# One full-height value product for the 16 meta keys of an attention head, and a 128-wide spread of the reciprocal sums

## The chip, the core and the metric

The kernel runs on one core of a Trainium2 chip. A core has a matrix engine (TensorE, PE in the rows; PEld is its loading of stationary operands), a vector engine (DVE), a scalar engine (ACT), a general engine (GpSimd, POOL) and a queue engine that issues transfers (SP). Matrix products are written to PSUM; all else lies in SBUF, 128 partitions wide. The metric is the device time of one execution in microseconds (us); less is better.

## The reference

A layer of a streaming encoder: 2048 tokens of width 1024, with 16 learned meta tokens in front (2064 rows). After a norm, one projection feeds eight heads of a recurrence (RWKV-7) and eight heads of forgetting attention; both results go through an output projection, and a gated feed-forward network with a short convolution follows. The change touches the attention alone:

```python
def block(args):                       # 128 queries at a time
    q_i, c_i, pos_i = args
    s = jnp.einsum('bhqd,bhkd->bhqk', q_i, k) + c_i[..., None] - c[:, :, None, :]
    s = jnp.where(kpos[None, :] <= pos_i[:, None], s, -jnp.inf)
    p = jax.nn.softmax(s, axis=-1)
    return jnp.einsum('bhqk,bhkd->bhqd', p, v)
...
o = o * jax.nn.sigmoid(og.astype(f32))
```

## The kernel before

All large products take each fp32 operand as two parts, a rounded high part (type fp32r) and the rest (low), and sum three products: high by high, high by low, low by high. The program is written in blocks, but the order of the instructions on each engine is made by a list scheduler when the program is built; it is fixed then. Instructions of one engine run in that order, and wait for the others by semaphores.

Attention is built three times. `at(0, True)` and `at(1, False)` take queries of the first half, with two buffers for a head's keys and values; `at2` takes the eight later query blocks, with one buffer. In each, `run` goes over eight heads. `load_head` (L876) brings a head's keys, queries and values; `vs` is the value tile, [keys, key block, 128], with the high part of the 64 value columns in its left half and the low part in its right half. Key block 0 holds the 16 meta keys, the others 128 keys each. `softmax` makes the unnormalised probabilities P of 128 queries. `value` (L971) takes a pair of query blocks (N = 256 columns, or 272 with the 16 meta queries): for every key block it transposes P on TensorE into `pt` (L995), splits it into `ph` on ACT (L1003) and `pl` on DVE (L1004), and adds two products to `o`, `ph` by `vs` and `pl` by `vs` (L1008). `value` runs 64 times: 8 heads by 2, 2 and 4 pairs. For block 0 both operands have 16 partitions only, so these products use 16 rows of the array.

Behind the products, the reciprocal of the softmax sum, a column per query, is brought into row form: GpSimd copies it 64 wide into `E` (L1019), TensorE transposes `E` into a PSUM tile of the scores' kind, `rp` (L1020), and ACT copies that to `rb` (L1023), which multiplies the output gate `og`.

While attention runs, the scheduler puts feed-forward and output-projection products between its own: helper line L1083 with the tiles `pp`, `ww_hi`, `ww_lo`, and `pj` (L203 to L205) of the last input projections.

Of the kernel before, what the change touches and what calls it, by code (L numbers as in the profile page):

```python
# [7 lines left out]
F32 = mybir.dt.float32  # L8
F32R = mybir.dt.float32r
AF = mybir.ActivationFunctionType  # L10
ALU = mybir.AluOpType
# [51 lines left out]
def pools(*args):  # L63

    *ps, where = args
    return lambda shape, tag, bufs=1, dt=F32: ps[where.get(tag, -1)](shape, tag, bufs, dt)
# [789 lines left out]
def attention(K, ctx, name, phases, bufs, banks):  # L856


    nc = K.nc
    sp = pools(*(Pool(K.tc, ctx, name + i, side="right") for i in "ab"), dict.fromkeys(("kl", "kq", "cb", "raw", "vs"), 0))  # L860
    ps = pools(*(Pool(K.tc, ctx, f"{name}ps{i}", PSUM, side="right") for i in range(3)), {"s": 0, "pt": 1})
    nhead, nP, nph, W, nraw, masks, kve = bufs
    ns, npt, no = banks
# [3 lines left out]
    NQ = max(sum(16 if i < 0 else 128 for i in qt) for bl in phases for qt in bl)  # L867
    pmask = False

    if masks:  # L870
        idr, cmr = (sp([128, 128], t, dt=F32R) for t in ("idr", "cmr"))
        nc.scalar.copy(idr, K.ident)
        nc.scalar.copy(cmr, K.cmask)

    def load_head(h, qa, nk_all):
        p_, hh = divmod(h, 2)  # L876
        r = slice(64 * hh, 64 * hh + 64)
        kl = sp([128, NK], "kl", nhead, F32R)[:, :nk_all]
        kq = sp([128, NK + NR], "kq", nhead, F32R)
        kh, qs = kq[:, :nk_all], kq[:, NK : NK + nk_all - qa]  # L880
        cb = sp([128, NK], "cb", nhead)[:, :nk_all]
        nc.sync.dma_start(cb, K.cd[h : h + 1, :nk_all].to_broadcast([128, nk_all]))
        raw_tile = lambda: sp([128, W], "raw", nraw)
        sub = (nc.vector if kve else nc.gpsimd).tensor_sub
        for a, b, both in pieces(qa, nk_all):
            n, t, u = b - a, slice(a, b), slice(a - qa, b - qa)
            raw = raw_tile()[:, : n * (1 + both)].rearrange("p (i t) -> p i t", t=n)
            for j in range(2):
                nc.sync.dma_start(raw[64 * j : 64 * j + 64], K.qk[p_, r, 0 : 1 + both, t])
            nc.scalar.copy(kh[:, t], raw[:, 0])  # L890
            sub(kl[:, t], raw[:, 0], kh[:, t].bitcast(F32))  # L891
            if both:
                nc.scalar.copy(qs[:, u], raw[:, 1])
                nc.gpsimd.tensor_sub(qs[64:128, u], raw[64:128, 1], qs[64:128, u].bitcast(F32))  # L894
        nt = (nk_all - 16) // 128 + 1
        vs = sp([128, (NK - 16) // 128 + 1, 128], "vs", nhead, F32R)
        for j in [0, *range(1, nt, W // 64)]:
            p, js = (16, 1) if j == 0 else (128, min(W // 64, nt - j))
            raw = raw_tile()[:p, : 64 * js].rearrange("p (j d) -> p j d", d=64)
            k0 = keys(j)[0]  # L900
            nc.sync.dma_start(raw, K.vn[k0 : k0 + p * js, 64 * h : 64 * h + 64].rearrange("(j p) d -> p j d", p=p))
            t = vs[:p, j : j + js]
            nc.scalar.copy(t[:, :, 0:64], raw)
            nc.gpsimd.tensor_sub(t[:, :, 64:128], raw, t[:, :, 0:64].bitcast(F32))
        og = sp([64, NR], "og", min(nhead, 2))[:, : nk_all - qa]
        nc.sync.dma_start(og, K.og[p_, r, qa:nk_all])
        return kh, kl, qs, cb, vs, og, qa

    def pieces(qa, nk):

        out = []
        for lo, hi, w in ((0, qa, W), (qa, nk, W // 2)):
            m = -(-(hi - lo) // w)
            w = -(-(hi - lo) // (16 * m)) * 16 if m else w
            out += [(a, min(a + w, hi), lo == qa) for a in range(lo, hi, w)]
        return out
# [52 lines left out]
    def keys(j):  # L969
        return (0, 16) if j == 0 else (16 + 128 * (j - 1), 128)  # L970

    def value(hd, qt, soft):

        vs, qa = hd[4], hd[6]
        nqs = [16 if i < 0 else 128 for i in qt]
        Ps, inv = zip(*soft)
        q0 = 0 if qt[0] < 0 else 16 + 128 * qt[0]
        N = sum(nqs)
        per = 2 if N <= 256 else 1
        shape = [128, per, 512 // per]  # L980
        o = ps([128, 512], "o", no)[:, :N]
        nt = qt[-1] + 2
        j = 0
        while j < nt:
            js = [j] if j == 0 else list(range(j, min(j + per, nt)))
            pt = ps(shape, "pt", npt)
            kn = keys(j)[1]
            ph, pl = sp(shape, "ph", nph, F32R), sp(shape, "pl", nph, F32R)
            cols = []
            for x, jj in enumerate(js):  # L990
                k0, kn = keys(jj)
                c0 = 0
                for P, i, nq in zip(Ps, qt, nqs):
                    if jj <= i + 1:
                        nc.tensor.transpose(pt[:kn, x, c0 : c0 + nq], P[:nq, k0 : k0 + kn], K.ident[:nq, :nq])  # L995
                    c0 += nq
                cols.append(sum(nq for i, nq in zip(qt, nqs) if jj > i + 1))
            if len(set(cols)) == 1:
                views = [(slice(0, len(js)), cols[0])]
            else:  # L1000
                views = [(slice(x, x + 1), c) for x, c in enumerate(cols)]
            for xs, c in views:
                nc.scalar.copy(ph[:kn, xs, c:N], pt[:kn, xs, c:N])  # L1003
                nc.vector.tensor_sub(pl[:kn, xs, c:N], pt[:kn, xs, c:N], ph[:kn, xs, c:N].bitcast(F32))  # L1004
            for x, jj in enumerate(js):
                c = cols[x]
                for y, pp in enumerate((ph, pl)):
                    nc.tensor.matmul(o[:, c:N], vs[:kn, jj], pp[:kn, x, c:N], start=jj == 0 and y == 0,  # L1008
                                     stop=jj == nt - 1 and y == 1)
            j += len(js)  # L1010
        o2 = sp([64, NQ], "o2", min(nhead, 2))[:, :N]
        nc.scalar.copy(o2, o[64:128])
        nc.vector.tensor_tensor(o2, o2, o[0:64], op=ALU.add)

        rp = ps([128, 512], "s", ns)[:64, :N]
        c0 = 0
        for r, nq in zip(inv, nqs):
            e = sp([128, 64], "E", 2)[:nq]
            nc.gpsimd.tensor_scalar(e, r.to_broadcast([nq, 64]), 1.0, 0.0, op0=ALU.mult, op1=ALU.add)  # L1019
            nc.tensor.transpose(rp[:, c0 : c0 + nq], e, K.ident[:nq, :nq])  # L1020
            c0 += nq
        rb = sp([64, NQ], "rb", min(nhead, 2))[:, :N]
        nc.scalar.copy(rb, rp)  # L1023
        og = hd[5][:, q0 - qa : q0 - qa + N]
        nc.gpsimd.tensor_tensor(og, og, rb, op=ALU.mult)
        nc.vector.tensor_tensor(og, o2, og, op=ALU.mult)

    def finish(hd, h, qt, soft, last):
        value(hd, qt, soft)
        if last:  # L1030
            p_, hh = divmod(h, 2)
            og, qa = hd[5:]
            nc.sync.dma_start(K.yd[4 + p_, 64 * hh : 64 * hh + 64, qa : qa + og.shape[1]], og)
# [176 lines left out]
def tail(K, ctx, at, c0):  # L1210
# [7 lines left out]
    with ExitStack() as c1:  # L1218
        gA = pools(*(Pool(tc, c1, f"ff{i}", side="left") for i in "ABCD"), {"acc": 0, "xh": 1, "xl": 2})
        bank = lambda shape: pA(shape, "pp", 3)  # L1220
        cvA = lambda: gA([128, 512], "cv", 5)
        early = [F.group(*g, dict(x=gA, a=gA, z=gA, out=bank, up=bank, ytag="x", abufs=1, parts=WHOLE, small=KC,
                                  cv=cvA, sq=cvA, stage=lambda i: lambda c: cvA())) for g in FGROUPS[:2]]
        early[0].parts = PARTS
        early[0].small = KC // 2
        early[1].small = 0
        F.w_o(early[0])
        at(1, False)
        c0.close()
        with ExitStack() as c2:  # L1230
            attention(K, c2, "at2", [[[2 * i, 2 * i + 1] for i in range(4, 8)]], (1, 4, 2, 352, 2, 0, 0), (2, 2, 1))(0, False)
        pR = Pool(tc, late, "ffpR", PSUM, side="right")
        bankR = lambda shape: pR(shape, "pr", 5)
        F.mlp(early[0])()
        F.w_o(early[1])
        rest = F.mlp(early[1], 8, bankR)
        R = Pool(tc, late, "ffR", side="right")

        def stage(i):
            t = R([128, KC, 514], "yh" if i else "yl")  # L1240
            return lambda c: t[:, c]

        gs = [F.group(*g, dict(x=R, a=R, abufs=1, out=bankR, up=bank, ytag="y", stage=stage, parts=WHOLE, small=KC,
                                   sq=lambda: R([128, 512], "sqv", 1))) for g in FGROUPS[2:]]
        F.w_o(gs[0])
        rest()
# [61 lines left out]
```

## Time and profile before

| | |
|---|---|
| median of 3 runs | 3463.3 us (3452.35 to 3463.97) |
| the profiled execution | 3458.59 us; its span 3456.7 us |
| mean granted TensorE clock in it | 0.989 |
| TensorE busy | 3351.8 us, 97% of the span |
| DVE, ACT, POOL busy | 2296.5, 1650.9, 1151.2 us |

The span runs from the first to the last instruction; 1.9 us of the profiled execution lie around it. Sums below are made against the profiled execution, and 4.7 us is what it lies below the median.

### The profile page before, as it was taken

To read this page: it belongs to the slowest core of one execution; us is meant where nothing else is said; L and a number is where in the kernel's file an instruction comes from. 1 tells how busy PE (TensorE), PEld (TensorE's weight loads), DVE (VectorE), ACT (ScalarE), POOL (GpSimd) and SP (SyncE) were. 2 spreads that over 40 slices of the span, in tenths; PEclk is the share of its full clock that TensorE was granted. 3 is DMA by queue.
4 is the path that set the end of the run, shared out by engine and by line. 5 is a ranking of instruction groups with operands and counts; after the bars stand their busy time and mean duration, and the time that the engine had idled before them with its cause. 6 is when DMAs were issued, how large, how long until landed. Compare 5 with 4: busy or idle time off the path is not lost.

```text
span 3456.7 us, 62711 instructions
## 1 busy us (share of the span) xinstructions
PE 3351.8 (97%) x23323; PEld 2950.0 (85%) x23323; DVE 2296.5 (66%) x4849; ACT 1650.9 (48%) x3426; POOL 1151.2 (33%) x2029
## 2 busy tenths in 40 slices
PE   7999999999999998999999999999999999999999
PEld 7889889988988987999999998888887888878887
DVE  5655666576566656887778776776664666646665
ACT  4543444554344466765666665555333333333332
POOL 4441113344111256744444344332214221132111
PEclk9999999999999999999999999999999999999999
DMA  4565343356534264333332353232324323232322
GB/s 113 120 140 148 96 108 87 102 121 146 147 96 104 79 180 135 114 99 103 93 89 82 92 160 94 91 100 86 121 92 146 104 92 98 88 120 93 97 92 92
DMA packets 352890, 376.60 MB, mean 109 GB/s; under 512 B 169112, under 2 KB 281992, under 8 KB 351560
## 3 DMA queue, kind: packets, MB, share of 16 engines
q1 hardware_dynamic: 352392, 372.52, 37.6%
q8 instruction: 184, 3.01, 0.4%
q14 instruction: 122, 1.00, 0.1%
q0 software_dynamic: 192, 0.07, 0.0%
HBM read 302.22 MB, written 70.27 MB: 108 GB/s over the span
## 4 chain that ended last, share of the span: by engine, by line
PE 50%; DMA 2%; issue 1%; POOL 1%; DVE 1%; ACT 1%; SPq 0%; POOLq 0%; ACTq 0%; DVEq 0%
PE pp L1083 30%; PE pr L1083 12%; PE o L1008 3%; PE pt L995 2%; PE s L946 1%; DMA raw<-d_qk 1%; PE s L948 1%; POOL kl L891 0%; DVE ww_lo L82 0%; DMA cb<-d_cd 0%; PE s L1020 0%; ACT ph L1003 0%; ACT P L965 0%; DVE P L939 0%; POOL kq L894 0%
## 5 line engine op out<-in xcount | busy, mean ns | idle before, releaser
L82 DVE TENSOR_TENSOR ww_lo<-ww_raw,ww_hi 128x1024 fp32r<-128x1024 f32 (+1 forms) x304 | 373.9, 1239 | 237.4 <-PE pp L1083 128.4
L81 ACT CAST ww_hi<-ww_raw 128x1024 fp32r<-128x1024 f32 (+1 forms) x304 | 307.4, 1024 | 392.9 <-PE pp L1083 147.9
L1083 PE MATMUL pp<-xh,ww_hi 128*128 128x512 f32 (+2 forms) x1952 | 431.4, 354 | 13.0 <-ACT xh L1144 4.7
L1083 PE MATMUL pp<-xl,ww_hi 128*128 128x512 f32 (+2 forms) x1952 | 431.7, 351 | 0.0
L1083 PE MATMUL pp<-xh,ww_lo 128*128 128x512 f32 (+2 forms) x1952 | 430.6, 351 | 0.0
L1083 PEld LDWEIGHTS pp<-xh,ww_hi 128*128 128x128 f32 x1952 | 325.4, 190 | 69.1 <-ACT xh L1144 9.8
L1083 PEld LDWEIGHTS pp<-xl,ww_hi 128*128 128x128 f32 x1952 | 328.7, 189 | 52.9
L1083 PEld LDWEIGHTS pp<-xh,ww_lo 128*128 128x128 f32 x1952 | 325.3, 189 | 46.8
L1166 POOL TENSOR_SCALAR c<-c,pc 128x1 f32<-128x1 f32 x220 | 82.4, 375 | 582.4 <-ACT c L1163 580.9
L1004 DVE TENSOR_TENSOR pl<-pt,ph 128x512 fp32r<-128x512 f32 (+4 forms) x416 | 220.6, 538 | 67.7 <-ACT ph L1003 63.4
L1003 ACT CAST ph<-pt 128x512 fp32r<-128x512 f32 (+4 forms) x416 | 189.3, 468 | 144.9 <-PE pt L995 105.8
L939 DVE CUSTOM_DVE_ANT_0 P<-cb,s 16x16 f32<-16x16 f32 (+8 forms) x360 | 183.0, 520 | 73.8 <-PE s L948 45.1
L1178 POOL TENSOR_TENSOR zl<-cv,zh 128x512 fp32r<-128x512 f32 (+1 forms) x110 | 122.2, 1111 | 300.0 <-ACT zh L1177 276.6
L1191 DVE TENSOR_TENSOR acc<-acc,pr 128x512 f32<-128x512 f32 x240 | 164.4, 688 | 81.3 <-PE pr L1083 76.9
L995 PE MATMUL pt<-cst,P 128*128 128x128 f32 (+2 forms) x1224 | 198.6, 276 | 3.1 <-DVE pl L1004 1.5
L1008 PE MATMUL o<-ph,vs 128*128 128x256 f32 (+3 forms) x640 | 188.5, 302 | 11.2 <-ACT ph L1003 6.8
L1160 ACT ACTIVATE cv<-pp,pc 128x510 f32<-128x510 f32 (+1 forms) x220 | 151.8, 691 | 84.0 <-PE pp L1083 82.3
L1008 PE MATMUL o<-pl,vs 128*128 128x256 f32 (+3 forms) x640 | 174.7, 290 | 5.0 <-DVE pl L1004 4.4
L89 POOL TENSOR_TENSOR wi<-sq,kx 128x320 fp32r<-128x320 f32 (+2 forms) x48 | 48.3, 1007 | 390.8 <-ACT kx L88 291.7
L203 PE MATMUL pj<-xah,w_hi 128*128 128x384 f32 x480 | 164.9, 344 | 1.7 <-ACT xah L194 1.7
L205 PE MATMUL pj<-xah,w_lo 128*128 128x384 f32 x480 | 163.3, 340 | 0.4 <-DVE w_lo L82 0.4
L204 PE MATMUL pj<-xal,w_hi 128*128 128x384 f32 x480 | 163.0, 340 | 0.0
(386 smaller groups left out, 8557.4 us busy)
## 6 DMA issues: line engine op xcount, KB each, us to landing
ww_raw<-in_fin_dram SPq DMA_DIRECT2D x176, 512.0 KB, 3.5
ww_raw<-in_fout_dram SPq DMA_DIRECT2D x88, 512.0 KB, 3.6
w_raw<-in_wt_dram SPq DMA_DIRECT2D x60, 512.0 KB, 3.7
xv<-d_var SPq DMA_DIRECT2D x32, 384.0 KB, 6.0
ww_raw<-in_wo_dram SPq DMA_DIRECT2D x24, 512.0 KB, 3.4
raw<-d_qk SPq DMA_DIRECT2D x112, 88.0 KB, 2.6
cb<-d_cd SPq DMA_DIRECT2D x8, 1032.0 KB, 8.2
out_dram<-acc SPq DMA_DIRECT2D x32, 256.0 KB, 2.9
```

Source lines behind the costliest of these rows:

```text
L81: nc.scalar.copy(hi, raw)
L82: nc.vector.tensor_sub(lo, raw, hi.bitcast(F32))
L203: nc.tensor.matmul(p, wh[:, c, :M], xh[:, c, :n], start=c == 0, stop=False)
L204: nc.tensor.matmul(p, wh[:, c, :M], xl[:, c, :n], start=False, stop=False)
L205: nc.tensor.matmul(p, wl[:, c, :M], xh[:, c, :n], start=False, stop=c == KC - 1)
L939: nc.vector.tensor_tensor_reduce(dst, c, src, 1.0, 3e38, op0=ALU.add, op1=ALU.min, accum_out=mx[:nq, np_ : np_ + 1])
L995: nc.tensor.transpose(pt[:kn, x, c0 : c0 + nq], P[:nq, k0 : k0 + kn], K.ident[:nq, :nq])
L1003: nc.scalar.copy(ph[:kn, xs, c:N], pt[:kn, xs, c:N])
L1004: nc.vector.tensor_sub(pl[:kn, xs, c:N], pt[:kn, xs, c:N], ph[:kn, xs, c:N].bitcast(F32))
L1008: nc.tensor.matmul(o[:, c:N], vs[:kn, jj], pp[:kn, x, c:N], start=jj == 0 and y == 0, stop=jj == nt - 1 and y == 1)
L1083: self.K.nc.tensor.matmul(p, w, x, start=i == 0, stop=i == len(mms) - 1)
L1191: nc.vector.tensor_tensor(a, a, p, op=ALU.add)
```

## The change

For key block 0, `value` no longer takes `ph` and `pl` from the ring. A tile `meta` of 128 partitions, cleared once per attention object, takes the high part in partitions 0 to 15 and the low part in 32 to 47. Plane 0 of `vs` is cleared on GpSimd for each head and holds the 16 value rows twice, in partitions 0 to 15 and, by one more ACT copy, in 32 to 47; all other partitions are zero. One product of 128 rows then stands for the two of 16 rows. `E` and the PSUM tile `rp` get 128 columns and 128 partitions; ACT reads the first 64 partitions as before.

```diff
+    meta = sp([128, NQ], "meta", dt=F32R)
+    nc.gpsimd.memset(meta.bitcast(F32), 0.0)
...
         vs = sp([128, (NK - 16) // 128 + 1, 128], "vs", nhead, F32R)
+        nc.gpsimd.memset(vs[:, 0].bitcast(F32), 0.0)
...
+        nc.scalar.copy(vs[32:48, 0], vs[0:16, 0].bitcast(F32))
...
-            ph, pl = sp(shape, "ph", nph, F32R), sp(shape, "pl", nph, F32R)
+            if j:
+                ph, pl = sp(shape, "ph", nph, F32R), sp(shape, "pl", nph, F32R)
...
+            if j == 0:
+                c, p0 = cols[0], meta
+                nc.scalar.copy(p0[:kn, c:N], pt[:kn, 0, c:N])
+                nc.vector.tensor_sub(p0[32 : 32 + kn, c:N], pt[:kn, 0, c:N], p0[:kn, c:N].bitcast(F32))
+                nc.tensor.matmul(o[:, c:N], vs[:, 0], p0[:, c:N], start=True, stop=False)
+                j = 1
+                continue
...
-                    nc.tensor.matmul(o[:, c:N], vs[:kn, jj], pp[:kn, x, c:N], start=jj == 0 and y == 0,
-                                     stop=jj == nt - 1 and y == 1)
+                    nc.tensor.matmul(o[:, c:N], vs[:kn, jj], pp[:kn, x, c:N], start=False, stop=jj == nt - 1 and y == 1)
...
-        rp = ps([128, 512], "s", ns)[:64, :N]
+        rp = ps([128, 512], "s", ns)[:, :N]
...
-            e = sp([128, 64], "E", 2)[:nq]
-            nc.gpsimd.tensor_scalar(e, r.to_broadcast([nq, 64]), 1.0, 0.0, op0=ALU.mult, op1=ALU.add)
+            e = sp([128, 128], "E", 2)[:nq]
+            nc.gpsimd.tensor_scalar(e, r.to_broadcast([nq, 128]), 1.0, 0.0, op0=ALU.mult, op1=ALU.add)
...
-        nc.scalar.copy(rb, rp)
+        nc.scalar.copy(rb, rp[:64])
```

On TensorE, in `at2`, the second pair of query blocks of its first head begins like this before; the first two rows with `o` are the two 16-row products on key block 0, and `pp` are feed-forward products.

```order
L1083 MATMUL pp_26185<-zl_25262,ww_hi_26071 128x258
L1083 MATMUL pp_26185<-zl_25432,ww_hi_26077 128x258
L1008 MATMUL o_18533<-ph_18535,vs_18282 128x256
L1008 MATMUL o_18533<-pl_18536,vs_18282 128x256
L1008 MATMUL o_18533<-ph_18544,vs_18282 128x256
L1083 MATMUL pp_26185<-zh_25261,ww_lo_26072 128x258
```

The same pair of query blocks with the change, on the same engine (L1096 is the feed-forward line there):

```order
L1096 MATMUL pp_26045<-zh_25121,ww_lo_25932 128x258
L1096 MATMUL pp_26045<-zh_25291,ww_lo_25938 128x258
L1013 MATMUL o_18472<-meta_18159,vs_18222 128x256
L1022 MATMUL o_18472<-ph_18480,vs_18222 128x256
L1022 MATMUL o_18472<-pl_18481,vs_18222 128x256
```

One product on `meta` stands where two stood, and the feed-forward products have moved by a few places; over the whole program TensorE has 64 matrix products fewer.

On GpSimd, in `at2`, where the value tile of the second head is filled, before (`cm` is the masked decay row of a score block, `zl` a feed-forward operand):

```order
L1178 TENSOR_TENSOR zl_26392<-cv_26496,zh_26391 128x258
L958 TENSOR_TENSOR cm_19216<-cb_18808,cst_72 128x128
L904 TENSOR_TENSOR vs_18867<-raw_18868,vs_18867 16x64
L904 TENSOR_TENSOR vs_18867<-raw_18872,vs_18867 128x5x64
L904 TENSOR_TENSOR vs_18867<-raw_18876,vs_18867 128x5x64
L1019 TENSOR_SCALAR E_19341<-nm_19079 128x64
```

And with the change:

```order
L1191 TENSOR_TENSOR zl_26252<-cv_26356,zh_26251 128x258
L964 TENSOR_TENSOR cm_19145<-cb_18741,cst_72 128x128
L900 MEMSET vs_18800 128x128
L908 TENSOR_TENSOR vs_18800<-raw_18806,vs_18800 128x5x64
L908 TENSOR_TENSOR vs_18800<-raw_18802,vs_18800 16x64
L1032 TENSOR_SCALAR E_19267<-nm_19011 128x128
```

The clearing stands ahead of the first writes into the value tile, and what follows it on GpSimd keeps nearly its order.

## Rows read from the trace of the kernel before

**Rows 1.** The page: busy time of the engines; the chain that ended last, by engine.

```profile
PE 3351.8 (97%) x23323; PEld 2950.0 (85%) x23323; DVE 2296.5 (66%) x4849; ACT 1650.9 (48%) x3426; POOL 1151.2 (33%) x2029
PE 50%; DMA 2%; issue 1%; POOL 1%; DVE 1%; ACT 1%; SPq 0%; POOLq 0%; ACTq 0%; DVEq 0%
```

**Rows 2.** Busy time by stretch: while attention runs.

```profile
core 0: us, PE busy (x) PEld busy (x) DVE busy (x) ACT busy (x) POOL busy (x), PEclk, DMA share, GB/s
1206.00:2406.00 1200.00, 1165.46 (x8070) 1066.30 (x8070) 899.07 (x2541) 728.98 (x1610) 563.39 (x1139) 0.99 0.36 107
```

**Rows 3.** TensorE's waits from 1206 to 2406 us, the longest (us in total, times, longest).

```profile
PE o L1008 <- ACT ph L1003: 6.8, 6, 2.3
```

**Rows 4.** TensorE's groups by shape: rows*columns of the stationary operand, then the moving one.

```profile
L1008 PE MATMUL o<-ph,vs 16*128 16x256 f32 x56 | 21.3, 380 | 0.9 <-DVE o L1013 0.7 <-DVE nm L964 0.2
L1020 PE MATMUL s<-cst,E 16*64 16x16 f32 x8 | 1.6, 204 | 0.0
```

**Rows 5.** TensorE in order of time (start, us, what): 16-row products, transposes.

```profile
1507.00 0.75 PE L1083 MATMUL pp<-xh,ww_hi 128*128 128x258 f32 x5
1507.69 0.38 PE L1008 MATMUL o<-ph,vs 16*128 16x256 f32 x1
1507.91 0.27 PE L1008 MATMUL o<-pl,vs 16*128 16x256 f32 x1
1508.11 0.38 PE L1008 MATMUL o<-ph,vs 128*128 128x256 f32 x1
1508.34 0.52 PE L1083 MATMUL pp<-xh,ww_hi 128*128 128x258 f32 x3
...
1509.54 0.49 PE L995 MATMUL pt<-cst,P 128*128 128x128 f32 x3
1509.78 0.37 PE L1083 MATMUL pp<-xl,ww_hi 128*128 128x258 f32 x1
1509.99 0.28 PE L1008 MATMUL o<-ph,vs 128*128 128x256 f32 x1
...
1511.91 1.01 PE L1083 MATMUL pp<-xh,ww_hi 128*128 128x258 f32 x7
1512.75 0.28 PE L1008 MATMUL o<-ph,vs 128*128 128x256 f32 x1
...
1513.41 0.38 PE L1020 MATMUL s<-cst,E 128*64 128x128 f32 x2
1513.55 0.36 PE L1083 MATMUL pp<-xl,ww_hi 128*128 128x258 f32 x1
1513.75 0.28 PE L1008 MATMUL o<-pl,vs 128*128 128x256 f32 x1
```

**Rows 6.** The same view: a 16-row product alone between full ones.

```profile
1549.95 0.99 PE L1083 MATMUL pp<-xh,ww_hi 128*128 128x258 f32 x7
1550.88 0.38 PE L1008 MATMUL o<-ph,vs 16*128 16x256 f32 x1
1551.19 0.39 PE L1083 MATMUL pp<-xh,ww_hi 128*128 128x258 f32 x1
1551.41 0.52 PE L1083 MATMUL pp<-xl,ww_hi 128*128 128x258 f32 x3
```

**Rows 7.** The same view: the first and the last 16-row product.

```profile
1221.69 0.59 PE L1008 MATMUL o<-ph,vs 16*128 16x272 f32 x1
...
2393.94 0.38 PE L1008 MATMUL o<-pl,vs 16*128 16x256 f32 x1
```

**Rows 8.** Groups by shape on GpSimd and ACT that are nearest to what is added.

```profile
L1019 POOL TENSOR_SCALAR E<-nm 128x64 f32<-128x64 f32 x128 | 38.7, 303 | 96.8 <-PE s L1020 52.9 <-DVE nm L966 31.6 <-PE pp L1083 5.5
L100 POOL TENSOR_SCALAR E<-r 128x128 f32<-128x128 f32 x14 | 6.9, 494 | 0.6
L794 POOL MEMSET Y<- 64x512 f32 x1 | 0.5, 524 | 0.1
L1003 ACT CAST ph<-pt 16x256 fp32r<-16x256 f32 x56 | 20.1, 359 | 23.4 <-PE pt L995 23.1
```

## The prediction, made before the changed kernel ran

> **What bounds the kernel now.** I read the page first: TensorE is busy for 3351.8 of 3456.7 us, DVE for 66%, and half of the chain that ended last is TensorE's; no other engine has over 2% of it [rows 1]. The reader is to see that work taken from TensorE is worth something only where TensorE works without a break. So I read the busy time of the stretch in which attention runs, from 1206 to 2406 us: TensorE 1165.46 of 1200.00 us, DVE 899.07, ACT 728.98, POOL 563.39 [rows 2]. TensorE stands idle for 34.5 us there, 3%; the longest sum of one kind of wait is 6.8 us, for ACT's split of P [rows 3]. The scheduler has put feed-forward products between those of attention, and so TensorE is the bound here too. The granted clock is 0.99 in this stretch, that is the level of 2.4 GHz nearly throughout, so no gain is to be looked for from the clock.
>
> A busy TensorE says little by itself, because the ends of products are modelled. What counts is the distance from one start to the next, and so I read TensorE in order of time around the products that the change touches.
>
> **The 16-row products.** `value` runs 64 times and issues two 16-row products each time, 128 in all, most of them 256 columns wide [rows 4]; the first starts at 1221.69 us, the last at 2393.94 us [rows 7]. Going through this view between the two, I count 77 uninterrupted runs of them: 51 times both together, 26 times one alone.
>
> The price of a run comes from starts. Plain products of 256 or 258 columns follow each other every 0.12 us: seven from 1511.91 to 1512.75 [rows 5]. Now the pair: from 1507.00 us (five plain products, the pair, one plain product) to 1508.34 us are 1.34 us for eight products, where 8 x 0.12 = 0.96 us would do: 0.38 us too much [rows 5]. In detail, the pair's first starts late by 0.69 - 0.60 = 0.09 us, its second comes 0.22 us after it, the next full one 0.20 us later, and the one behind that 0.23 us later: each of the four steps loses about 0.1 us. A 16-row product alone: from 1549.95 to 1551.41 us are 1.46 us for nine products, against 1.08 us: again 0.38 us too much [rows 6]. So a run costs 0.38 us above its own products, one or two in it.
>
> With the change no value product has 16 rows. Removed: 77 x 0.38 = 29.3 us of lost steps, and 64 products (two become one) x 0.12 = 7.7 us. Together **37.0 us** of TensorE's time. The new product has 128 rows and 256 columns, like the plain ones, and I give it their 0.12 us.
>
> **The 128-wide `E`.** The 64-wide transposes use half the columns of the array. At 1513.41 us two of them start, the next product at 1513.55 and the one behind it at 1513.75 us: 0.34 us for two transposes and a product. For three full transposes and a product the rows give 1509.54 to 1509.99 us, 0.45 us, and the third transpose accounts for the 0.11 us between the two [rows 5]. There is no room for 0.38 us in the 0.34, so fewer columns cost nothing where fewer rows do, and a wider `E` gives TensorE nothing: 0 us. The eight transposes of the 16 meta queries keep 16 rows [rows 4]; they may at most grow to the price of a run, 8 x 0.38 = 3.0 us, at least stay as they are. I take 0, since the rows of their operand don't change.
>
> The Trainium skill, page TensorEngine Tiling (Array Packing), section Tiling Modes, Key Properties, says that a change of the tiling mode drains TensorE. The trace agrees for rows, with the 0.38 us above, and does not show it for columns. By the rule alone the 64-wide transposes would pay like the 16-row products; that is the third rival below.
>
> **What is added, and what hides it.** On GpSimd the 128 copies into `E` grow from 303 ns towards the 494 ns of a 128x128 copy, 128 x 0.19 = 24.4 us, and 24 clearings of `vs` (8 heads x 3) come, at no more than the 0.52 us of a 64x512 one, 12.6 us, with two of `meta` beside them, 1.0 us [rows 8]. That is 38 us on an engine with 637 us of idle time in this stretch [rows 2]. On ACT 24 copies of 16x128 come, at no more than the 0.36 us of a 16x256 one: 8.6 us beside 471 us of idle time [rows 2, 8]. The copy and the subtraction into `meta` take the place of equal ones into `ph` and `pl`. Cover for all of it is TensorE's queue of feed-forward products. If the cover were gone, only the wider `E` stands in front of TensorE in every `value`: two copies by 0.19 us by 64 is the same 24.4 us, the loss at its worst. I take 0.
>
> A new wait: the one product on `meta` waits for both ACT and DVE, where the first of two waited for ACT alone. In the new order some forty products stand between the 16-row transposes and this product, about as before, so the split (0.36 us on ACT and a like time on DVE) has some 4 us to end in. The single `meta` must be read by one `value` before the next writes it; a `value` starts every 1200 / 64 = 19 us, so this is never late.
>
> **The sum.** 3458.6 us, less up to 37.0 us. Not all of it will arrive: DVE, ACT and the transfers don't get faster, the order is fixed, and where TensorE comes earlier it waits a little more. The lower bound is TensorE's share of the chain, 50% [rows 1]: 18.5 us. The upper is all, 37.0 us. I am nearer to the upper, because the stretch itself shows TensorE busy for 97% [rows 2], and take 5 us off, that is the idle time there growing from 34.5 to some 40 us: a gain of 32 us. That gives 3426.6 us against the profiled execution. The median of the runs lies 4.7 us above it and the lowest run 6 us below, so I add half of the 4.7 and forecast **3429 us**, 1% less than the 3463.3 us.
>
> **The rivals.** First, *attention is held by its other engines*: the time TensorE wins turns into waits for the splits on DVE and ACT. For it speaks that DVE is busy for 75% of the stretch and that these waits exist [rows 2, 3]; against it that they come to few us in 1200. It would give between nothing and the chain's share, 3440 to 3463 us.
>
> Second, *slower*: the clearing of `vs` in `at2`. There `vs` has one buffer, so the clearing waits for the last product of the head before, and stands on GpSimd ahead of `E`, the masks `cm` and the feed-forward parts `zl`; while it waits, TensorE runs out of operands. Before, ACT's first copy into `vs` had that wait. The rest of the change gains 32 us, so with eight heads in `at2` each clearing must stop TensorE for over 4 us to end slower; at 7 us it would be 3429 + 8 x 7 = 3485 us. Against it: GpSimd has more idle time than any engine here, and the clearing stands where the first value copies stood.
>
> Third, *columns cost too*: some 76 runs of 64-wide transposes would give back 76 x 0.38 = 29 us more, 3400 us. The rows at 1513.41 us speak against it [rows 5]. This is what the rule on tiling modes would give.
>
> Fourth, the scheduler's order: it differs from attention on. I can't price it from rows; I let it widen the range by some 8 us on either side.
>
> **How the numbers follow.** The forecast, gains of 24 to 42 us: 0.69. Held by other engines: 0.21, of which 0.07 is still over 0.5%. Clearing: 0.06, of which 0.05 slower and 0.01 about even. Columns: 0.04. About 0.5% (17 us) is what a measurement of this kernel can tell from no change. Faster: 0.69 + 0.07 + 0.04 = 0.80; the same: 0.14 + 0.01 = 0.15; slower 0.05. The range: below, all 37 us from the profiled time and 8 us of luck in the order, 3414; above, the chain's share from the median, 3445, and a few us of disorder, 3450.
>
> **What the profile after would show.** Right: no value product of 16 rows; starts 0.12 us apart around the products on `meta`; 64-wide forms gone, and the steps behind the transposes as before (0.34 us for two and a product); the stretch of attention shorter by some 30 us, what comes after it as long as before; TensorE's idle time in it about 40 us. Wrong, if TensorE's waits for ACT, DVE or GpSimd in that stretch grow by over 15 us, or if a full-height product on `meta` still has steps of 0.2 us around it.

## Result and the profile after

The changed kernel takes 3424.6 us (median of 4 runs, 3421.39 to 3433.38) against 3462.8 us before (4 runs): a ratio of 0.9893, 95% interval 0.9876 to 0.991. The forecast of 3429 us was 4.4 us too high. The profiled execution takes 3421.68 us, its span is 3419.8 us and its mean granted clock 0.987, so 36.9 us are to be found between the two profiles.

The page of the changed kernel: busy time of the engines, and the chain that ended last, by engine.

```profile
PE 3321.0 (97%) x23259; PEld 2941.8 (86%) x23259; DVE 2301.7 (67%) x4849; ACT 1653.1 (48%) x3450; POOL 1165.1 (34%) x2055
PE 51%; DVE 2%; DMA 2%; POOL 2%; issue 2%; ACT 2%; SPq 0%; POOLq 0%; ACTq 0%; DVEq 0%
```

TensorE has 64 products fewer and is 30.8 us less busy than in [rows 1]; GpSimd has 13.9 us more work, ACT 2.2 us more. The bound is the same.

Busy time by stretch in the changed kernel (length, then PE, PEld, DVE, ACT and POOL with their counts, the granted clock, DMA share, GB/s): the stretch of [rows 2], then from the first attention score to the last value product, what follows, and both together.

```profile
1206.00:2406.00 1200.00, 1166.99 (x8165) 1084.02 (x8165) 928.10 (x2569) 743.83 (x1651) 593.07 (x1177) 0.99 0.38 113
1206.00:2338.00 1132.00, 1098.99 (x7873) 1029.26 (x7873) 881.08 (x2508) 715.96 (x1610) 568.76 (x1137) 0.99 0.37 110
2338.00:3419.00 1081.00, 1070.86 (x4573) 859.99 (x4572) 673.75 (x921) 390.12 (x571) 257.68 (x557) 1.00 0.33 105
1206.00:3419.00 2213.00, 2169.85 (x12445) 1889.25 (x12444) 1554.84 (x3428) 1106.08 (x2181) 826.45 (x1693) 0.99 0.35 107
```

The last three rows answer to these of the kernel before, which the forecast had not read:

```profile
2406.00:3456.00 1050.00, 1038.78 (x4439) 834.82 (x4437) 650.11 (x887) 375.58 (x547) 248.93 (x530) 1.00 0.32 104
1206.00:3456.00 2250.00, 2204.24 (x12507) 1901.12 (x12506) 1549.18 (x3428) 1104.55 (x2157) 812.33 (x1669) 0.99 0.34 106
```

From the first score on, 2250 us have become 2213: 34.4 us of it is busy time (2204.24 less 2169.85), 2.6 us idle time (45.8 became 43.2). Attention ends 68 us earlier, near 2336 us, and what follows is 31 us longer: the scheduler put 134 products (4573 less 4439) behind attention that stood inside it before. So one must not read the gain from the attention stretch alone.

TensorE in order of time (start, length of the group, what): a product on `meta` among plain ones, and two transposes of `E`.

```profile
1507.44 0.41 PE L1096 MATMUL pp<-zh,ww_hi 128*128 128x258 f32 x2
1507.68 0.41 PE L1096 MATMUL pp<-zl,ww_hi 128*128 128x258 f32 x2
1507.93 0.41 PE L1096 MATMUL pp<-zh,ww_lo 128*128 128x258 f32 x2
1508.17 0.29 PE L1013 MATMUL o<-meta,vs 128*128 128x256 f32 x1
1508.29 0.28 PE L1022 MATMUL o<-ph,vs 128*128 128x256 f32 x1
1508.41 0.60 PE L1002 MATMUL pt<-cst,P 128*128 128x128 f32 x4
...
1613.98 0.38 PE L1033 MATMUL s<-cst,E 128*128 128x128 f32 x2
1614.12 0.36 PE L1022 MATMUL o<-ph,vs 128*128 128x256 f32 x1
1614.32 0.40 PE L1096 MATMUL pp<-zh,ww_hi 128*128 128x256 f32 x2
```

From 1507.44 to 1508.41 us are 0.97 us for eight products; [rows 5] has 1.34 us for eight with the pair in them. Two full transposes and a product take 1613.98 to 1614.32, 0.34 us, the same as two 64-wide ones in [rows 5].

Groups by shape of the changed kernel (count, then busy time, mean ns of one, idle time before them and what ended it), which answer to [rows 4] and [rows 8]:

```profile
L1013 PE MATMUL o<-meta,vs 128*128 128x256 f32 x56 | 17.3, 309 | 5.7 <-DVE meta L1012 3.1 <-POOL edge L1180 2.6
L1032 POOL TENSOR_SCALAR E<-nm 128x128 f32<-128x128 f32 x128 | 47.6, 374 | 85.6 <-PE s L1033 59.4 <-DVE nm L972 13.9 <-DVE pl L1018 5.9
L910 ACT CAST vs<-vs 16x128 fp32r<-16x128 f32 x24 | 7.1, 298 | 5.2 <-POOL vs L908 4.6
L900 POOL MEMSET vs<- 128x128 f32 x24 | 4.9, 205 | 10.6 <-PE o L1022 10.0 <-DMA ww_raw<-in_fin_dram 0.5
```

Some of TensorE's waits in the changed kernel from 1206 to 2410 us (total, times, longest): the first is the longest and answers to [rows 3], the others are taken up again below.

```profile
PE o L1022 <- ACT ph L1017: 5.2, 5, 3.6
PE o L1013 <- DVE meta L1012: 3.1, 2, 2.3
PE o L1013 <- POOL edge L1180: 2.6, 1, 2.6
PE s L952 <- DVE mx L945: 1.2, 3, 0.7
PE s L952 <- POOL kq L897: 1.1, 1, 1.1
PE pt L1002 <- DVE meta L1012: 1.0, 2, 0.5
```

### The profile page after: what moved, and what is told of

It is laid out like the page before. It is cut to its first block, busy times and chain, and to the rows that moved or that the text cites. A ratio compares the mean times of both kernels' runs of the same rounds, so it can differ in the third digit from the quotient of the medians.

```text
span 3419.8 us, 62536 instructions
## 1 busy us (share of the span) xinstructions
PE 3321.0 (97%) x23259; PEld 2941.8 (86%) x23259; DVE 2301.7 (67%) x4849; ACT 1653.1 (48%) x3450; POOL 1165.1 (34%) x2055
## 4 chain that ended last, share of the span: by engine, by line
PE 51%; DVE 2%; DMA 2%; POOL 2%; issue 2%; ACT 2%; SPq 0%; POOLq 0%; ACTq 0%; DVEq 0%
PE pp L1096 30%; PE pr L1096 12%; PE o L1022 3%; PE pt L1002 3%; DMA raw<-d_qk 2%; PE s L952 1%; PE s L954 1%; DVE ww_lo L82 1%; POOL xl L1158 0%; POOL kl L894 0%; DVE P L945 0%; DVE pl L1018 0%; ACT P L971 0%; DMA cb<-d_cd 0%; ACT ph L1017 0%
## 5 line engine op out<-in xcount | busy, mean ns | idle before, releaser
L1096 PE MATMUL pp<-xh,ww_hi 128*128 128x512 f32 (+2 forms) x1952 | 432.3, 353 | 11.4 <-ACT xh L1157 6.0
L1096 PE MATMUL pp<-xh,ww_lo 128*128 128x512 f32 (+2 forms) x1952 | 429.1, 351 | 0.0
L1096 PE MATMUL pp<-xl,ww_hi 128*128 128x512 f32 (+2 forms) x1952 | 428.4, 350 | 0.3 <-POOL xl L1158 0.3
L1096 PEld LDWEIGHTS pp<-xh,ww_hi 128*128 128x128 f32 x1952 | 324.8, 190 | 66.5 <-ACT xh L1157 11.1
L1096 PEld LDWEIGHTS pp<-xl,ww_hi 128*128 128x128 f32 x1952 | 326.2, 189 | 52.8 <-POOL xl L1158 1.0
L1096 PEld LDWEIGHTS pp<-xh,ww_lo 128*128 128x128 f32 x1952 | 325.3, 189 | 47.4
L1018 DVE TENSOR_TENSOR pl<-pt,ph 128x512 fp32r<-128x512 f32 (+2 forms) x352 | 196.1, 562 | 51.7 <-ACT ph L1017 50.1
L1017 ACT CAST ph<-pt 128x512 fp32r<-128x512 f32 (+2 forms) x352 | 167.8, 486 | 103.4 <-PE pt L1002 72.9
L1177 DVE SCALAR_TENSOR_TENSOR cv<-pp,pc,cv 128x511 f32<-128x511 f32 (+1 forms) x220 | 140.7, 639 | 36.0 <-ACT c L1176 35.9
L1022 PE MATMUL o<-ph,vs 128*128 128x256 f32 x576 | 158.1, 284 | 5.5 <-ACT ph L1017 5.2
```

Source lines behind the costliest of these rows:

```text
L1096: self.K.nc.tensor.matmul(p, w, x, start=i == 0, stop=i == len(mms) - 1)
```

## The experiments

The theory, *rows*: the whole gain is the 16-row products' price on TensorE; `E`'s width gives nothing. Its rivals at the start: *columns* (a product that fills only 64 columns has a price too) and *other engines hold it*. A third, *order*, stands in the expectations of e2 and e5 and came to the front after the first four runs: programs with the same products differ by the order that the scheduler gives them. Each run is compared with runs of the kernel before on the same chip (medians 3463.2, 3463.4 and 3463.3 us in the three groups).

### The parts apart

**e1: the change with `E` 64 wide.** Edits here and below are against the changed kernel where nothing else is said. Where the width of `E` changes, the lines of `rp`, of the GpSimd copy and of `rb` follow it and are in part left out.

```diff
-        rp = ps([128, 512], "s", ns)[:, :N]
+        rp = ps([128, 512], "s", ns)[:64, :N]
...
-            e = sp([128, 128], "E", 2)[:nq]
+            e = sp([128, 64], "E", 2)[:nq]
```

> The full-height product on meta alone; E and its transposes stay 64 wide. Rows theory (a run of 16-row products costs 0.38 us above its own products, columns cost nothing): as fast as the changed kernel, a ratio of 0.989 to the kernel before, within 0.3%. Columns theory (64-wide transposes cost a run's price too): some of the gain is lost, up to 136 transposes' runs, so 0.992 or slower if a tenth of the gain came from them.

Measured: 3445.6 us, ratio 0.9953 (0.9939 to 0.9968). Less than half of the gain: the rows theory missed.

**e2: `E` 128 wide in the kernel before; the 16-row products stay.**

```diff
-            e = sp([128, 64], "E", 2)[:nq]
+            e = sp([128, 128], "E", 2)[:nq]
```

> E and its transposes 128 wide alone; the two 16-row products stay (78 runs in the new order). Rows theory: no change, 0.998 to 1.003. Columns theory: faster by what the columns cost, up to 29 us, 0.992. Order theory (any new order from the scheduler could have given the gain): nothing definite, but a gain of 1% here would speak for it.

Measured: 3464.7 us, ratio 1.0007 (0.9991 to 1.0024). A wide `E` by itself gives nothing. So the parts give 17.6 and -1.5 us (3463.19 less 3445.57 and 3464.65), together 16, and both at once 38: something is in the sum that belongs to neither.

**e5: everything of the change but the full height.** The high part lies in `meta`, the low part in the ring, and two products use 16 rows each.

```diff
+                p1 = sp(shape, "pl", nph, F32R)[:kn, 0]
...
-                nc.tensor.matmul(o[:, c:N], vs[:, 0], p0[:, c:N], start=True, stop=False)
+                nc.tensor.matmul(o[:, c:N], vs[:kn, 0], p0[:kn, c:N], start=True, stop=False)
+                nc.tensor.matmul(o[:, c:N], vs[:kn, 0], p1[:, c:N], start=False, stop=False)
```

> As the changed kernel, but the high part in meta and the low part in a ring tile go through two 16-row products again, in 78 runs; the clearing, the added copy, the 128-wide E, and the high part off the ring all stay. Rows theory: the whole gain is lost, ratio 0.998 to 1.003. Order or ring theory (the gain comes from the scheduler's new order or from the ring tile that is no longer taken): a good part stays, 0.994 or less.

Measured: 3460.5 us, ratio 0.9985 (0.9972 to 0.9998). The clearing, the copy and the wide `E` are all there, and nearly all of the gain is gone, so it does not come from them. Two things are missing here at once, the single product in place of two and its full height; e4 parts them.

**e4: one product in place of two, on the first 48 partitions only.**

```diff
-                nc.tensor.matmul(o[:, c:N], vs[:, 0], p0[:, c:N], start=True, stop=False)
+                nc.tensor.matmul(o[:, c:N], vs[:48, 0], p0[:48, c:N], start=True, stop=False)
```

> As the changed kernel, but the one product on meta takes the first 48 partitions only, which is a 64-row tile of the array; it stands in 64 runs of its own. One product stands for two, all additions of the change are there, only its height is less. Rows theory: the 7.7 us of the removed products and 77 less 64 runs (13 x 0.38 = 4.9 us) are won, 64 x 0.38 = 24.3 us are not: 3450 us, ratio 0.996. Rival (the gain is one product instead of two, or less work on the rings, and not the height): as the changed kernel, 0.989.

Measured: 3438.8 us, ratio 0.9926 (0.9911 to 0.9941), between the two: 11 us under the 3450 us of the rows theory. TensorE in order of time in this kernel:

```profile
1516.84 0.41 PE L1096 MATMUL pp<-zh,ww_hi 128*128 128x258 f32 x2
1517.08 0.41 PE L1096 MATMUL pp<-zl,ww_hi 128*128 128x258 f32 x2
1517.33 0.40 PE L1096 MATMUL pp<-zh,ww_lo 128*128 128x258 f32 x2
1517.66 0.38 PE L1013 MATMUL o<-meta,vs 48*128 48x256 f32 x1
1517.97 0.39 PE L1022 MATMUL o<-ph,vs 128*128 128x256 f32 x1
1518.20 0.60 PE L1002 MATMUL pt<-cst,P 128*128 128x128 f32 x4
```

From 1516.84 to 1518.20 us are 1.36 us where the changed kernel needs 0.97: 0.39 us too much, as for 16 rows. Padding to 48 partitions doesn't save the price, padding to 128 does.

In the two traces the instructions of TensorE, DVE, ACT and GpSimd stand in the same order (by line, operation and tiles), so e4 and the changed kernel differ by the height of 64 products alone. From 1206 us to the end, in e4:

```profile
1206.00:3438.00 2232.00, 2193.64 (x12470) 1898.33 (x12468) 1556.27 (x3430) 1109.71 (x2187) 827.17 (x1695) 0.99 0.34 107
```

TensorE is busy for 23.8 us more than in the changed kernel (64 x 0.39 = 25 us would be the price) and idle for 38.4 us in place of 43.2, 4.8 us less. The spans differ by 18.9 us, the medians by 14.2 (3438.83 less 3424.62): this is what the full height is worth in the change's own order. Against the kernel before, e4 is busy for 10.6 us less, where the rows theory has 7.7 + 4.9 = 12.6, and idle for 7.4 us less. No height explains those 7.4 us; the order of the two programs differs.

### Columns or order

**e8: e1 with `E` 65 wide**, so that the transposes use more than 64 columns. The order of the instructions is that of e1 on TensorE, DVE, ACT and GpSimd.

```diff
-            e = sp([128, 64], "E", 2)[:nq]
+            e = sp([128, 65], "E", 2)[:nq]
```

> As e1 (the full-height product on meta alone), with E and its transposes 65 wide instead of 64, so that they use all columns of the array. On every engine the order of the instructions is e1's, to the last one. Columns theory (what e1 lacks against the changed kernel is the price of 64-wide transposes): as the changed kernel, a ratio of 0.989. Order theory (e1 lacks it because of its own order, whose waits are 15 us longer): as e1, 0.995, within 0.2%; the steps behind the transposes stay as they were.

Measured: 3445.9 us, ratio 0.9953 (0.9937 to 0.9968), e1's to a digit. Columns have no price here. The Trainium skill, page TensorEngine Tiling (Array Packing), section Tiling Modes, Key Properties, says that a change of the tiling mode drains TensorE, and the section Tiling Modes lists 128x64 among the modes. e4 agrees for rows, with 0.39 us at 48 of them; e1 against e8 shows no loss for these transposes of 64 columns, and no run here shows in which mode they ran.

**e9: `E` copied 128 wide, transposed 64 wide.** The copies on GpSimd and the buffers' sizes are the changed kernel's, the order is another.

```diff
-            nc.tensor.transpose(rp[:, c0 : c0 + nq], e, K.ident[:nq, :nq])
+            nc.tensor.transpose(rp[:, c0 : c0 + nq], e[:, :64], K.ident[:nq, :nq])
```

> As the changed kernel, with E still 128 wide on GpSimd, but only 64 of its columns transposed; the scheduler gives it an order of its own. Columns theory: slower than the changed kernel by as much as e1, 0.995. Order theory: the same work on TensorE as the changed kernel and e1 in a third order, so between 0.985 and 0.996, by its idle time alone.

Measured: 3444.0 us, ratio 0.9947 (0.9932 to 0.9963). Neither the width of the copies nor that of the buffer brings the gain.

### The price of 16 rows in one and the same order

**e3 and e3r: e1 and one more product a `value`, of zeros**, which adds nothing to `o`: in e3 of full height, in e3r on 16 rows. The order of the two is the same.

```diff
+    none = sp([128, 128], "none", dt=F32R)
+    nc.gpsimd.memset(none.bitcast(F32), 0.0)
...
+                nc.tensor.matmul(o[:, c:N], none, p0[:, c:N], start=False, stop=False)
```
```diff
+                nc.tensor.matmul(o[:, c:N], none[:16], p0[:16, c:N], start=False, stop=False)
```

> As e1, with one more product of full height for each value: a tile of zeros by meta, added to the same sum, which leaves the result as it is. Rows theory: 64 x 0.12 = 7.7 us of TensorE's time more than e1, whose order it does not share: 0.9975, within 0.4%. It is the partner of e3r.

> As e3, with the added product on the first 16 partitions of the same two tiles, so that it uses 16 rows of the array. Same number of instructions, same order on every engine, same tiles; only the height differs. Rows theory: 64 runs x 0.38 = 24.3 us slower than e3, that is 0.7%. Rivals (the height of a product costs nothing by itself): as e3, within 0.2%.

Measured: 3448.0 us, 0.9963 (0.9949 to 0.9977), and 3461.9 us, 1.0002 (0.9985 to 1.0018). TensorE in order of time, first e3, then e3r:

```profile
1510.76 0.64 PE L1099 MATMUL pp<-xh,ww_lo 128*128 128x258 f32 x4
1511.23 0.28 PE L1015 MATMUL o<-meta,vs 128*128 128x256 f32 x1
1511.35 0.28 PE L1016 MATMUL o<-meta,none 128*128 128x256 f32 x1
1511.47 0.28 PE L1025 MATMUL o<-ph,vs 128*128 128x256 f32 x1
1511.59 0.60 PE L1004 MATMUL pt<-cst,P 128*128 128x128 f32 x4
```
```profile
1527.87 0.64 PE L1099 MATMUL pp<-xh,ww_lo 128*128 128x258 f32 x4
1528.35 0.28 PE L1015 MATMUL o<-meta,vs 128*128 128x256 f32 x1
1528.56 0.38 PE L1016 MATMUL o<-meta,none 16*128 16x256 f32 x1
1528.87 0.39 PE L1025 MATMUL o<-ph,vs 128*128 128x256 f32 x1
1529.10 0.60 PE L1004 MATMUL pt<-cst,P 128*128 128x128 f32 x4
```

The same seven products take 0.83 and 1.23 us: 0.40 us for a run, 64 x 0.40 = 26 us in all. But the medians differ by only 13.9 us. Busy time from the first score (1206.9 us in e3, 1214.0 us in e3r) to the end shows why, first e3, then e3r:

```profile
1206.90:3445.20 2238.30, 2180.32 (x12504) 1901.33 (x12501) 1559.10 (x3428) 1106.89 (x2181) 815.22 (x1695) 0.99 0.35 106
```
```profile
1214.00:3465.30 2251.30, 2204.05 (x12504) 1909.70 (x12501) 1561.16 (x3428) 1107.15 (x2181) 817.69 (x1695) 0.99 0.34 106
```

TensorE is busy for 23.7 us more in e3r, and idle for 47.3 us in place of 58.0. So 10.7 of the 23.7 us lie in time in which TensorE would have waited for others, and 13.0 us are left.

### More orders

**e10, e11, e12: the changed kernel with `E` 96, 112 and 120 wide; e13: the kernel before with `E` 96 wide.** All use more than 64 columns; each has an order of its own, and e11's is nearest to the changed kernel's. The edit of e10 (the others differ by the number, e13 has it in the kernel before):

```diff
-        rp = ps([128, 512], "s", ns)[:, :N]
+        rp = ps([128, 512], "s", ns)[:96, :N]
...
-            e = sp([128, 128], "E", 2)[:nq]
+            e = sp([128, 96], "E", 2)[:nq]
```

> The changed kernel with the spread E 96 columns wide in place of 128, all else as in the change: the same products on TensorE but for the transposes' columns, another order of the instructions. Order theory (the change found an order with some 13 us less waiting of TensorE than the other three orders with the same products, by chance): a draw of its own, ratio to the kernel before between 0.988 and 0.996 (3422 to 3449 us), and the difference to the changed kernel lies in TensorE's idle time (39 us in the changed kernel, 52 to 54 us in the three others, from the first attention score on). Rival (a 128-wide spread is worth something by itself): 0.995 as with 64 and 65 columns, with idle time as in the changed kernel. The 16-row price stays gone in both: no lost steps around the products on meta.

> The same with E 112 columns wide; its order on TensorE is the one nearest to the changed kernel's of the three widths. Order theory: nearer to the changed kernel than the others, 0.989 to 0.992 (3425 to 3436 us), idle time of TensorE 38 to 46 us from the first attention score on. Rival (a 128-wide spread is worth something by itself): 0.995, 3446 us.

> The same with E 120 columns wide, in an order that parts from the changed kernel's early. Order theory: a draw between 0.988 and 0.996 (3422 to 3449 us), differing by idle time. Rival (a 128-wide spread is worth something by itself): 0.995, 3446 us.

> The kernel before, its two 16-row products kept, with E 96 columns wide: one more order with the 16-row products in it. Order theory: as the other orders with 16-row products, 0.998 to 1.003 (3456 to 3474 us), and so the whole spread by order among kernels with these products is smaller than among those without. Rival (the order alone can give what the change gave): a ratio under 0.995 with the 16-row products still there.

Measured, with all others but e3 and e3r, which have a product more; idle is TensorE's from 1206 us to the end of one profiled execution, length less busy time as above (the first score starts between 1204 and 1218 us in all of them):

| kernel | median, us | ratio (95%) | span of the profile, us | idle, us |
|---|---|---|---|---|
| **16-row products** | | | | |
| before | 3463.3 | 1 | 3456.7 | 45.8 |
| e2 | 3464.7 | 1.0007 (0.9991 to 1.0024) | 3464.4 | 43.7 |
| e13 | 3463.7 | 0.9997 (0.9984 to 1.0009) | 3463.2 | 45.2 |
| e5 | 3460.5 | 0.9985 (0.9972 to 0.9998) | 3448.8 | 44.9 |
| **one of 48 rows**: e4 | 3438.8 | 0.9926 (0.9911 to 0.9941) | 3438.7 | 38.4 |
| **full height only** | | | | |
| the change | 3424.6 | 0.9893 (0.9876 to 0.991) | 3419.8 | 43.2 |
| e11 | 3422.1 | 0.989 (0.9872 to 0.9907) | 3432.7 | 45.2 |
| e12 | 3433.3 | 0.9917 (0.99 to 0.9934) | 3429.2 | 48.0 |
| e1, e8 (one order) | 3445.6, 3445.9 | 0.9953, 0.9953 | 3438.0, 3445.4 | 59.3, 57.3 |
| e9 | 3444.0 | 0.9947 (0.9932 to 0.9963) | 3446.1 | 56.8 |
| e10 | 3444.6 | 0.9948 (0.9936 to 0.996) | 3447.1 | 61.8 |

The order theory holds: six orders with the same products on TensorE lie between 3422 and 3446 us, and those above 3440 are those in which TensorE waits 57 to 62 us in place of 43 to 48. No 128-wide `E` is needed for the low end: e11 has 112, and is not to be told from the change. (Its profiled run is the slowest of its five; its attention starts 10 us late, the first value product at 1233.3 us against 1223.1.) Orders with 16-row products all lie between 3460 and 3465 us.

A part of the 24 us goes with TensorE's mean granted clock, which changes from run to run: e12 alone reaches from 3421.8 us at 0.989 to 3440.8 at 0.982. Among the runs at 0.985 to 0.987 the change, e11 and e12 take 3421 to 3435 us, and e1, e8, e9 and e10 take 3440 to 3451 us. The means are 15 us apart, and that much is left to the order.

The rows of busy time behind the idle column, of e1, of e10 and of e11:

```profile
1206.00:3438.00 2232.00, 2172.74 (x12444) 1889.47 (x12442) 1554.29 (x3428) 1109.00 (x2181) 822.81 (x1693) 0.99 0.34 107
```
```profile
1206.00:3447.00 2241.00, 2179.17 (x12455) 1897.08 (x12453) 1557.62 (x3428) 1109.89 (x2185) 826.74 (x1695) 0.99 0.34 106
```
```profile
1206.00:3432.00 2226.00, 2180.78 (x12545) 1900.67 (x12543) 1559.73 (x3438) 1109.61 (x2191) 830.79 (x1699) 0.99 0.35 108
```

Of the 18.2 us between the spans of e1 and the change, 16.1 are idle time. TensorE's waits in e1 from 1206 to 2410 us that are longer than in the changed kernel:

```profile
PE s L952 <- DVE mx L945: 7.1, 9, 2.1
PE s L952 <- POOL kq L897: 4.8, 5, 1.6
PE pp L1096 <- ACT ww_hi L81: 4.2, 2, 2.7
PE pt L1002 <- DVE meta L1012: 4.0, 3, 2.7
PE pp L103 <- POOL E L100: 3.7, 1, 3.7
```

They sum to 23.8 us over 20 waits, where the first, second and fourth come to 3.3 us in the changed kernel and the other two are not in its list; others are shorter in e1. No one wait names the difference: TensorE comes a little too early at many places, for scores (`s`), for weights of the feed-forward (`ww_hi`) and for the split into `meta`.

## Why the prediction was right, and where it was not

**TensorE as the bound, and the 37.0 us of its time: right.** From the first score on TensorE's busy time fell by 34.4 us and the window by 37.0. That the window meets the sum to a digit is luck: 2.6 us of it are idle time, which the prediction expected to grow. The run's price of 0.38 us is 0.40 in e3r and 0.39 in e4, and around the product on `meta` it is gone. That it is the height that counts is shown by two pairs in one order each, e3 against e3r and e4 against the change; e5 shows that the other parts of the change give next to nothing by themselves.

**`E` worth 0 us: right.** e2 by itself, and e8 against e1 in one order.

**What is added lies beside other work: right, and smaller than its bounds.** The copies into `E` take 374 ns in place of 303, 9.1 us more in all, not 24.4; ACT's extra copies 7.1 us, not 8.6. The product on `meta` waited for DVE 3.1 us in two waits, and the profile puts one wait of 2.6 us down to GpSimd, to a feed-forward operation (`edge`) and not to added work. The clearing that was to stop TensorE in every head shows no such loss: before all 24 clearings together GpSimd waited 10.0 us for value products.

**"Take 5 us off" for longer waits: the term depends on the order, and a second term was left out.** In the changed kernel the idle time did not grow but fell by 2.6 us. The loss that the prediction reasoned is there: in the change's own order, from 48 rows to full height, 4.8 of 23.8 us go into waits, near the 5 us. In e3's order it is 10.7 of 23.7. In the order of e1 and e8 the idle time lies 13.5 and 11.5 us above the kernel before, in those of e9 and e10 11.0 and 16.0. What the sum did not have is a gain from the new order: e4 waits 7.4 us less than the kernel before, and 7.4 less 4.8 are the 2.6 us. (Each idle time is that of one execution; e1 and e8, in one order, differ by 2.0 us.) So the forecast was near, and all of the 37 us arrived, because this order gave back what the waits took; that part is luck.

**The scheduler's order as 8 us on either side: too small on the upper side.** Among the orders with full-height products the medians reach from 3422 to 3446 us, 7 us below the forecast and 17 above it, and the change is at the low end. The time that the first rival gave, 3440 to 3463 us, came true in three of the six orders, so 0.21 looks low for it; but e1's longer waits are for scores and weights too, and not only for the splits of P that this rival named. All six lie inside the range that was given.

**"What comes after it as long as before": wrong.** It is 31 us longer, since feed-forward products moved behind attention; the stretch of attention is 68 us shorter, not 30.

What stays open: why some orders wait less than others. Order and waits go together in all kernels run, but no run changed the order at one place alone, so no single instruction can be named; that the change would keep its 38 us after another edit nearby can't be expected.

## What to carry to other kernels

A product on few rows between full ones costs more than its columns: look at the distances of starts around it, and pad the stationary and the moving operand with zeros to all 128 partitions when the time lies there; 48 did not do here. Where a scheduler sets the order, measure an edit in several orders that do the same work (a harmless width will give them) before the last half per cent is put down to the edit. And split the expected gain into what the bounding engine saves and what its waits will take back: here the second was a fifth of the first in one order and nearly half in another. When single runs differ, look at their granted clock before the order is named.

## What was not expected of the hardware

A product on 48 partitions between full ones costs the same 0.39 us a run as one on 16 [rows 5]. Transposes that fill 64 columns of the array cost the same as those that fill 65 or 128 (e1 against e8, and 0.34 us for two and a product with either). A copy of a broadcast column into `E` takes 374 ns in the mean for 128 columns in the changed kernel and 325 ns in e9, and for 64 columns 303 ns in the kernel before and 257 ns in e1: its mean depends on the program by some 50 ns, nearly as much as the 64 further columns cost.
